# Latent attention: the order of the second head's products and the place of the exponential table load

## The chip, the cores and the metric

The kernel runs on one core of one Trainium2 chip. The metric is the device time of one execution in microseconds (us). The engines are TensorE (PE, with its weight loads shown apart as PEld), VectorE (DVE), ScalarE (ACT), GpSimd (POOL) and SyncE (SP, which here only issues the loads of weights).

## The reference, cut to what matters

Two layers of a trunk over 512 tokens of width 1024. Each layer normalises, runs three token mixers side by side (neighbourhood attention, latent attention, windowed attention with sinks), gates and adds them, projects out, and then runs a convolutional feed-forward block. The change touches the latent attention and the start of the feed-forward block's down projection:

```python
def mla_attention(c_q, c_kv, k_rope, g_qa, g_kva, w_uq, w_ukv, cos, sin):
    q = (rmsnorm(c_q, g_qa) @ w_uq).reshape(B, S, H, MLA_QK)      # 4 heads, 128 + 64 wide
    q_nope, q_pe = q[..., :128], apply_rope(q[..., 128:], cos, sin)
    kv = (rmsnorm(c_kv, g_kva) @ w_ukv).reshape(B, S, H, 256)
    k_nope, v = kv[..., :128], kv[..., 128:]
    ...
        s = (qn @ k_nope + qp @ k_pe) * scale                     # per block of 128 queries, per head
        p = softmax(s)
        return p @ v

def conv_ffn(h, w_up, conv_w, conv_b, w_down):
    ...
    return (gelu(g) * a) @ w_down

for l in range(2):
    h = rmsnorm(x, norm1_g[l]); x = x + gated_parallel_mixer(h, ...)
    h = rmsnorm(x, norm2_g[l]); x = x + conv_ffn(h, ...)
```

The gates are sigmoid(h @ w_gate + b), which the kernel computes with a hyperbolic tangent.

## The kernel before, in words

Every float32 product is made of three matmuls on split operands (a high part and a low part, lines 161 to 163): ACT casts the high part (line 147) and DVE subtracts it to get the low part (line 148). Weights come through a ring: three raw tiles (`raw`), three tiles of high parts (`whi`) and three of low parts (`wlo`). The method `weights` hands out the next weight and calls `fetch`, which writes down the load and the split of a weight three steps ahead; so these splits stand in the program where an earlier weight is taken, and they carry a priority 300 steps ahead of their place.

The order of PE and of SP is written out by hand: `schedule` builds a list of items, and `run` calls `do_` plus the item's name for each. The instructions of ACT and DVE are put in order by a planner when the kernel is built: it takes, by its own clock, the earliest instruction in the program among those whose inputs are there, with a bonus of 300 steps for weight splits and of 100 for the items of attention (`ATTN`). On the chip each engine then runs its list strictly in that order.

The part that the change touches, in the order of PE before:

- `qr`: the rotary queries of all four heads. `rope` and `stack` (lines 210 to 220) turn each pair of heads into four tiles `qr`.
- `("qn", 0)` and `("kn", 0)`: the first head's queries and keys, 9 and 6 matmuls. `do_kn` scales the keys into `ev` (line 154) and then splits them (lines 147, 148).
- a gate, 24 matmuls into one PSUM bank. DVE empties that bank with one multiply (`gz`, line 154), and ACT runs the tangent (line 664).
- `("qn", 1)` and `("kn", 1)`: the second head's queries and keys, 9 and 6 matmuls.
- `("ms", 0, 0)` and `("ms", 0, 1)`: the first head's scores, two tiles of 128 queries each; a tile is 5 matmuls (lines 490 to 494). Then DVE finds the row maximum (`nm`, line 496), ACT the exponential (line 498), DVE the reciprocal (line 499), and ACT scales (line 500).
- another gate, 24 matmuls.

The scores have three PSUM banks, 2, 3 and 4 (`s=[2, 3, 4]` in `do_mla_attn`), handed out in turn, so the fourth tile takes bank 2 again and has to wait until the first tile's exponential has read it. Ahead of that, the products of `lat4`, `kr`, `v`, `qr`, `qn`, `kn` and the gate take the banks 4, 5, 0, 1, 2, 3 in turn, by which the gate's product lies in bank 2. So the first tile of scores has to wait until `gz` has emptied bank 2. `mla_attn` only hands out the banks anew and issues nothing.

The build puts a table load into ACT's list ahead of the first instruction that needs another table than the one loaded. The trace has four of them, and none ahead of a tangent, which runs after either of the two tables. One is at the start (line 85, before a small exponential on a column of ones), one at the first gelu of each layer (line 851), and one at the first exponential of the second layer's latent attention (line 498).

Of the kernel before, what the change touches and what calls it, by code (L numbers as in the profile page):

```python
# [13 lines left out]
AF = mybir.ActivationFunctionType  # L14
# [28 lines left out]
def r32(ap):  # L43
    return ap.bitcast(F32)
# [14 lines left out]
class Trunk:  # L59
# [5 lines left out]
    def __init__(self, ctx, tc, d):  # L65
        self.tc, self.nc, self.d, self.ctx = tc, tc.nc, d, ctx
        nc = self.nc
        self.small = ctx.enter_context(tc.tile_pool(name="small", bufs=1))
        self.const = ctx.enter_context(tc.tile_pool(name="const", bufs=1))
        self.wp = ctx.enter_context(tc.tile_pool(name="wp", bufs=1))  # L70
        self.psum = ctx.enter_context(tc.tile_pool(name="psum", bufs=1, space=bass.MemoryType.PSUM))
        self.groups, self.turn = {}, {}
        c = self.const
        self.x = [c.tile([P, S], F32, name=f"x{k}") for k in range(KD)]
        self.par = [self.small.tile([P, NPC], F32, name=f"par{l}") for l in range(L)]
        nc.scalar.dma_start(self.par[0], d["par"][0])
        self.early = c.tile([P, P], F32, tag="acc", name="early")
        nc.vector.memset(self.early, 1.0)
        self.idf = c.tile([P, P], F32, name="idf")
        make_identity(nc, self.idf)  # L80
        cst = self.small.tile([P, 6], F32, name="cst")
        self.neghalf, self.ones = cst[:, 0:4], cst[:, 4:5]
        nc.vector.memset(self.neghalf, -0.5)
        nc.vector.memset(self.ones, 1.0)
        nc.scalar.activation(cst[:, 5:6], self.ones, AF.Exp)
        self.idb = self.small.tile([P, P], BF16, name="idb")
        nc.vector.tensor_copy(self.idb, self.idf)
        self.specs, self.raws, self.parts, self.used = [], [], [], 0
        self.plans = [self.schedule(l) for l in range(L)]
        for s, W in self.plans:  # L90
            self.specs += [w for item in s for w in W.get(item, ())]
        nc.sync.dma_start(self.x[0], d["xT"][0:P, :])
        self.fetch(1, 0)
        for k in range(1, KD):
            if k == 4:
                self.fetch(3, 0)
            nc.sync.dma_start(self.x[k], d["xT"][k * P:(k + 1) * P, :])
        self.gmask = self.small.tile([P, 2 * P], BF16, name="gmask")
# [138 lines left out]
    def schedule(self, l):  # L237
        d = self.d
        w_in, w_uq, w_ukv = d["w_in"][l], d["w_uq"][l], d["w_ukv"][l]
        W = {}  # L240
        halves = lambda w, cs: [(w, 512 * hf, 4, c, P) for hf in range(2) for c in cs]
        W["lat"] = halves(w_in, [OFF_CQ + i * P for i in LAT])
        W["lat4"] = [(w_in, 0, KD, OFF_CQ + 4 * P, P)]
        W["kr"] = [(w_in, 0, KD, OFF_KR, 64)]
        W["v", 0] = [(w_ukv, 0, 2, 512, 512)]
        W["qr"] = [(w_uq, 0, 3, 512, 256)]
        for h in range(4):
            W["qn", h] = [(w_uq, 0, 3, h * P, P)]
            W["kn", h] = [(w_ukv, 0, 2, h * P, P)]
        for p in range(4):  # L250
            for i, n in enumerate("qkv"):
                W["na" + n, p] = [(w_in, 0, KD, 512 * i + p * P, P)]
        W["gk"] = [(w_in, 0, KD, OFF_GK, P)]
        W["gv"] = [(w_in, 0, KD, OFF_GV, P)]
        for i in range(4):
            W["gq", i] = [(w_in, 0, KD, OFF_GQ + i * P, P)]
        for b in range(3):
            for m in range(KD):
                W["gate", b, m] = [(w_in, 0, KD, OFF_GATE + b * D + m * P, P)]
                W["br", b, m] = [(d["w_br"][b][l], 0, 4, m * P, P)]  # L260
        W["br012"] = W["br", 2, 0] + W["br", 2, 1] + W["br", 2, 2]
        W["out"] = halves(d["w_out"][l], [m * P for m in range(4)])
        for m in range(4, KD):
            W["out", m] = [(d["w_out"][l], 0, KD, m * P, P)]
        ups = [p * NF + f for f in range(NF) for p in range(2)]
        W["up"] = halves(d["w_up"][l], [f * P for f in ups[:4]])
        for f in ups[4:]:
            W["up", f] = [(d["w_up"][l], 0, KD, f * P, P)]
        for g in range(2):
            W["down", g] = [(d["w_down"][l], k0 * P, nk, (4 * g + m) * P, P)  # L270
                            for k0, nk in ((0, 8), (8, 8), (16, 6)) for m in range(4)]

        gate = iter([("gate", b, m) for b in (1, 0, 2) for m in range(8)]).__next__
        s = ["mla_open", "lat", "lat4", "rs_q", "kr", "rb_q", "rs_k", ("v", 0), ("v", 1), "rb_k", "qr"]
        s += [("qn", 0), ("kn", 0), gate(), "mla_attn", ("qn", 1), ("kn", 1), ("ms", 0, 0), ("ms", 0, 1), gate()]
        for h in range(3):
            dn = [("qn", h + 2), ("kn", h + 2)] if h < 2 else [("naq", 0)]
            s += [("ms", h + 1, 0), ("mt", h, 0)] + dn + [("mp", h, 0), ("mt", h, 1), ("ms", h + 1, 1), ("mp", h, 1)]
        s += [gate(), ("mt", 3, 0), ("nak", 0), ("mp", 3, 0), ("mt", 3, 1), ("nav", 0), ("mp", 3, 1)]
        s += ["na_open", ("nvt", 0), ("ns", 0), ("naq", 1), ("ns", 1), ("nav", 1), ("br", 1, 0), ("nt", 0)]  # L280
        s += [("nak", 1), ("np", 0), ("nt", 1), ("br", 1, 1), gate(), ("np", 1)]
        for p in (1, 2):
            h = 2 * p
            s += [("nvt", p), ("ns", h), ("naq", p + 1), ("ns", h + 1), ("nav", p + 1), ("nt", h)]
            s += [("nak", p + 1), ("np", h), ("nt", h + 1), ("br", 1, p + 1), gate(), ("np", h + 1)]
        s += [("nvt", 3), ("ns", 6), ("br", 1, 4), gate(), ("ns", 7), ("br", 1, 5), gate(), ("nt", 6)]
        s += [("br", 1, 6), gate(), ("np", 6), ("nt", 7), ("br", 1, 7), gate(), ("np", 7)]
        s += ["gq_open", "gk", ("gq", 0), "gv", ("gq", 1), "gvt", gate(), ("br", 0, 0), ("br", 0, 1)]
        s += [("gs", 0, 0), ("gq", 2), ("gs", 0, 1), ("gq", 3)]
        for i in range(7):  # L290
            s += [("gt", i, 0), ("gt", i, 1), ("gs", i + 1, 0), ("br", 0, i + 1) if i else gate(), ("gp", i)]
            s += [("gs", i + 1, 1), gate()]
        s += [("gt", 7, 0), ("gt", 7, 1), gate(), ("gp", 7), "br012", ("br", 2, 3)]
        for m in range(4, 8):
            s += [gate(), ("br", 2, m)]
        s += ["out"] + [("out", m) for m in range(4, KD)]
        s += ["up"] + [("up", f) for f in ups[4:]]
        s += [("down", 0), ("down", 1)]
        return s, W
# [558 lines left out]
    def do_down(self, g):  # L858
        nc = self.nc
# [4 lines left out]
        ps = [self.bank("g") for _ in range(4)]  # L864
        last = self.l == L - 1
        if g == 0 and not last:
            self.norm_begin()
        if g == 0 and last:
            self.acc, self.ntags, self.xg = None, ["acc", "sq0", "sq1"], []
# [169 lines left out]
```

## Time and profile before

| | us |
|---|---|
| median of 3 runs | 1739.96 |
| lowest and highest of them | 1739.75, 1740.38 |
| the profiled execution | 1738.54 |
| its span, first to last instruction | 1736.7 |
| PE busy in the span | 1720.7 |
| DVE, ACT busy | 1157.6, 860.8 |

The profile is of one execution. Its rows give the start and the length of instructions from the span's start. Matmuls are pipelined: a matmul of 512 columns is 0.39 us long in the rows, but the next one starts some 0.23 us after it; that step is called a slot below. A number in square brackets is the idle time of the engine ahead of the instruction, and what ended it.

### The profile page before, as it was taken

The page shows a single profiled execution, that of the slowest core. Times are in us where ns is not written, and L with a number is a line of the kernel's source. Part 1 is how long each engine was busy: PE and PEld are TensorE (multiplying, and loading weights), DVE is VectorE, ACT ScalarE, POOL GpSimd, SP SyncE. Part 2 cuts the span into 40 slices and gives each one's busy share as a digit, 9 for nine tenths or more (in the row PEclk, how much of TensorE's full clock was granted, in tenths as well). Part 3 has the DMA queues.
Part 4 walks back from the last instruction along what each step waited for, and adds up shares of the span by engine and source line. Part 5 has one row for each costly group of instructions (what it writes and reads, how often), then busy time and mean ns, then how long its engine had stood idle before and what let it go on. Part 6 is the DMA issues. An engine that isn't in the chain of part 4 may idle for free.

```text
span 1736.7 us, 21596 instructions
## 1 busy us (share of the span) xinstructions
PE 1720.7 (99%) x8146; PEld 1431.7 (82%) x8146; DVE 1157.6 (67%) x1872; ACT 860.8 (50%) x1499; POOL 35.2 (2%) x90
## 2 busy tenths in 40 slices
PE   9999999999999999999999999999999999999998
PEld 7788888888888888888887888888888888888887
DVE  6767875887558777734357688768765587777234
ACT  5865655664345444423248656456644354444232
POOL 1010000000000000000010100000000000000000
PEclk9999999999999999999999999999999999999999
DMA  5222233222333333333232232332233333333231
GB/s 174 70 81 79 80 92 85 73 68 68 97 98 109 97 97 97 97 89 106 80 85 76 73 89 67 109 86 61 62 85 104 93 108 98 97 98 97 85 103 67
DMA packets 290696, 155.40 MB, mean 89 GB/s; under 512 B 8672, under 2 KB 287072, under 8 KB 290592
## 3 DMA queue, kind: packets, MB, share of 16 engines
q1 hardware_dynamic: 288288, 148.92, 30.1%
q0 software_dynamic: 2016, 4.72, 0.9%
q8 instruction: 64, 1.05, 0.3%
q10 hardware_dynamic: 288, 0.38, 0.1%
q14 instruction: 40, 0.33, 0.1%
HBM read 151.89 MB, written 2.10 MB: 89 GB/s over the span
## 4 chain that ended last, share of the span: by engine, by line
PE 93%; DVE 3%; ACT 2%; issue 1%; DMA 0%; SPq 0%; POOLq 0%; POOL 0%; DVEq 0%; ACTq 0%
PE ps_d L161 21%; PE ps_d L162 20%; PE ps_d L163 20%; PE ps_g L162 7%; PE ps_g L163 7%; PE ps_g L161 7%; PE ps_po L648 1%; PE ps_tp L783 1%; PE ps_tp L634 1%; DVE wlo L148 1%; PE ps_tp L507 1%; ACT rsw L210 1%; PE ps_s L755 1%; PE ps_s L616 0%; PE ps_d L422 0%
## 5 line engine op out<-in xcount | busy, mean ns | idle before, releaser
L147 ACT CAST whi<-raw 128x1024 fp32r<-128x1024 f32 (+4 forms) x340 | 302.4, 890 | 615.5 <-PE ps_d L162 341.1
L161 PE MATMUL ps_d<-hh,whi 128*128 128x512 f32 x1328 | 520.5, 392 | 0.0
L163 PE MATMUL ps_d<-hh,wlo 128*128 128x512 f32 x1328 | 517.4, 390 | 0.3 <-DVE wlo L148 0.3
L162 PE MATMUL ps_d<-hl,whi 128*128 128x512 f32 x1328 | 516.9, 389 | 0.0
L148 DVE TENSOR_TENSOR wlo<-raw,whi 128x1024 fp32r<-128x1024 f32 (+4 forms) x338 | 345.1, 1022 | 199.1 <-ACT whi L147 198.8
L163 PEld LDWEIGHTS ps_d<-hh,wlo 128*128 128x128 f32 x1328 | 249.3, 188 | 53.6 <-DVE wlo L148 1.2
L161 PEld LDWEIGHTS ps_d<-hh,whi 128*128 128x128 f32 x1328 | 249.5, 188 | 50.5 <-DVE rot L154 0.6
L162 PEld LDWEIGHTS ps_d<-hl,whi 128*128 128x128 f32 x1328 | 249.5, 188 | 50.1
L161 PE MATMUL ps_g<-ff,whi 128*128 128x512 f32 x334 | 129.9, 389 | 0.0
L162 PE MATMUL ps_g<-ff,whi 128*128 128x512 f32 x334 | 129.9, 389 | 0.0
L163 PE MATMUL ps_g<-ff,wlo 128*128 128x512 f32 x334 | 129.9, 389 | 0.0
L154 DVE TENSOR_TENSOR u<-ps_d,rb 128x512 f32<-128x512 f32 x80 | 55.3, 692 | 64.6 <-PE ps_d L163 64.6
L154 DVE TENSOR_TENSOR gz<-ps_d,rb 128x512 f32<-128x512 f32 x48 | 33.2, 692 | 81.4 <-PE ps_d L163 81.2
L845 ACT ACTIVATE c<-u,par 128x512 f32<-128x512 f32 x88 | 71.9, 817 | 4.8 <-DVE u L154 2.8
L162 PEld LDWEIGHTS ps_g<-ff,whi 128*128 128x128 f32 x334 | 62.7, 188 | 13.1
L148 DVE TENSOR_TENSOR pl<-ps_tp,ph 128x512 fp32r<-128x512 f32 x104 | 69.0, 684 | 6.7 <-ACT ph L147 6.6
L161 PEld LDWEIGHTS ps_g<-ff,whi 128*128 128x128 f32 x334 | 62.7, 188 | 13.0
L163 PEld LDWEIGHTS ps_g<-ff,wlo 128*128 128x128 f32 x334 | 62.7, 188 | 12.9
L847 DVE SCALAR_TENSOR_TENSOR c<-u,par,c 128x511 f32<-128x511 f32 x88 | 66.0, 751 | 2.7
L851 ACT ACTIVATE c<-c 128x512 f32<-128x512 f32 x44 | 27.8, 632 | 77.2 <-DVE c L847 77.2
L846 DVE SCALAR_TENSOR_TENSOR c<-u,par,c 128x511 f32<-128x511 f32 x88 | 65.6, 746 | 0.6 <-ACT c L845 0.6
L147 ACT CAST ph<-ps_tp 128x512 fp32r<-128x512 f32 x104 | 57.6, 586 | 5.9 <-PE ps_tp L507 2.8
(286 smaller groups left out, 2651.5 us busy)
## 6 DMA issues: line engine op xcount, KB each, us to landing
raw<-in_w_in_dram SPq DMA_DIRECT2D x86, 512.0 KB, 4.0
raw<-in_w_up_dram SPq DMA_DIRECT2D x80, 512.0 KB, 3.8
raw<-in_w_down_dram SPq DMA_DIRECT2D x32, 512.0 KB, 3.8
raw<-in_w_down_dram SPq DMA_DIRECT2D x16, 384.0 KB, 3.3
raw<-in_w_in_dram SPq DMA_DIRECT2D x18, 256.0 KB, 2.9
raw<-in_w_br_mla_dram SPq DMA_DIRECT2D x16, 256.0 KB, 2.8
raw<-in_w_br_na_dram SPq DMA_DIRECT2D x16, 256.0 KB, 2.8
raw<-in_w_br_gqa_dram SPq DMA_DIRECT2D x16, 256.0 KB, 2.8
```

The costliest lines, as they stand in the source:

```text
L147: nc.scalar.copy(hi, src)
L148: nc.vector.tensor_sub(lo, src, r32(hi))
L154: self.nc.vector.tensor_tensor(out, a, b, ALU.mult)
L161: mm(ps, sh, mh, start=first and k == 0, stop=False)
L162: mm(ps, sh, ml, start=False, stop=False)
L163: mm(ps, sl, mh, start=False, stop=last and k == n - 1)
L210: nc.scalar.copy(sw[32 * i:32 * i + 32, :], ps[32 * j:32 * j + 32, :])
L507: self.nc.tensor.transpose(tp[:, b * P:(b + 1) * P], self.pts[h, b][:, kc * P:(kc + 1) * P], self.idf)
L845: nc.scalar.activation(c, u, AF.Identity, bias=pr[:, PC_CB + fi:PC_CB + fi + 1], scale=cw[:, 1:2])
L846: nc.vector.scalar_tensor_tensor(c[:, 1:], u[:, :S - 1], cw[:, 0:1], c[:, 1:], ALU.mult, ALU.add)
L847: nc.vector.scalar_tensor_tensor(c[:, :S - 1], u[:, 1:], cw[:, 2:3], c[:, :S - 1], ALU.mult, ALU.add)
L851: nc.scalar.activation(c, c, AF.Gelu_apprx_tanh)
```

## The change

In `schedule`, the first half of the first head's scores, `("ms", 0, 0)`, moves ahead of `("qn", 1)` and `("kn", 1)`; the second half stays behind them. This holds in both layers. In `do_down`, once in the kernel (first layer, first half of the down projection), ACT is given an exponential on one column. Its input is the last gelu product's high part, multiplied by zero, and its output is a column that nothing reads. `self.warm` names the column that the exponential at the start already wrote to.

```diff
-        nc.scalar.activation(cst[:, 5:6], self.ones, AF.Exp)
+        self.warm = cst[:, 5:6]
+        nc.scalar.activation(self.warm, self.ones, AF.Exp)
...
-        s += [("qn", 0), ("kn", 0), gate(), "mla_attn", ("qn", 1), ("kn", 1), ("ms", 0, 0), ("ms", 0, 1), gate()]
+        s += [("qn", 0), ("kn", 0), gate(), "mla_attn", ("ms", 0, 0), ("qn", 1), ("kn", 1), ("ms", 0, 1), gate()]
...
         if g == 0 and not last:
+            nc.scalar.activation(self.warm, r32(self.ff[-1][0])[:, 0:1], AF.Exp, scale=0.0)
             self.norm_begin()
```

## Rows read from the trace of the kernel before

**Rows 1.** The page: busy time of each engine, share of the span, instructions.

```profile
PE 1720.7 (99%) x8146; PEld 1431.7 (82%) x8146; DVE 1157.6 (67%) x1872; ACT 860.8 (50%) x1499; POOL 35.2 (2%) x90
```

**Rows 2.** Waits of PE: tile, releaser: total us, times, longest us.

```profile
PE ps_s L490 <- ACT pt L498: 4.3, 2, 2.6
...
PE ps_s L490 <- DVE gz L154: 0.5, 2, 0.2
```

**Rows 3.** Timeline of PE, first layer: start, length, instruction, [idle before].

```profile
61.21 0.39 PE L163 MATMUL ps_d<-hh,wlo 128*128 128x512 f32 x1
...
64.61 0.39 PE L163 MATMUL ps_d<-yah,wlo 128*128 128x512 f32 x1
65.24 0.47 PE L490 MATMUL ps_s<-kn,qn 128*128 128x512 f32 x1 [0.25 <-DVE gz L154]
...
67.60 0.39 PE L490 MATMUL ps_s<-kn,qn 128*128 128x512 f32 x1
...
70.54 0.50 PE L490 MATMUL ps_s<-kn,qn 128*128 128x512 f32 x1 [1.65 <-ACT pt L498]
...
71.80 0.39 PE L161 MATMUL ps_d<-hh,whi 128*128 128x512 f32 x1
```

**Rows 4.** Timeline of PE, the same place in the second layer.

```profile
923.32 0.47 PE L490 MATMUL ps_s<-kn,qn 128*128 128x512 f32 x1 [0.24 <-DVE gz L154]
...
925.71 0.39 PE L490 MATMUL ps_s<-kn,qn 128*128 128x512 f32 x1
...
929.61 0.50 PE L490 MATMUL ps_s<-kn,qn 128*128 128x512 f32 x1 [2.61 <-ACT pt L498]
...
930.88 0.40 PE L161 MATMUL ps_d<-hh,whi 128*128 128x512 f32 x1
```

**Rows 5.** Timeline of DVE, first layer, around the first tile of scores.

```profile
61.52 1.41 DVE L220 TENSOR_TENSOR qr<-rot,qr 64x512 fp32r<-64x512 f32 x2
62.96 0.69 DVE L148 TENSOR_TENSOR kn<-ev,kn 128x512 fp32r<-128x512 f32 x1
63.69 0.69 DVE L220 TENSOR_TENSOR qr<-rot,qr 64x512 fp32r<-64x512 f32 x1
64.41 0.69 DVE L154 TENSOR_TENSOR gz<-ps_d,rb 128x512 f32<-128x512 f32 x1
...
65.85 1.70 DVE L148 TENSOR_TENSOR wlo<-raw,whi 128x1024 fp32r<-128x1024 f32 x2
...
68.99 1.28 DVE L496 TENSOR_REDUCE nm<-ps_s 128x1 f32<-128x512 f32 x2
```

**Rows 6.** Timeline of DVE, the same multiply in the second layer.

```profile
922.48 0.69 DVE L154 TENSOR_TENSOR gz<-ps_d,rb 128x512 f32<-128x512 f32 x1
```

**Rows 7.** Timeline of ACT, second layer: the table load and the first exponential.

```profile
927.49 1.28 ACT L498 ACT_TABLE_LOAD   x1
928.78 0.69 ACT L498 ACTIVATE pt<-ps_s,nm 128x512 f32<-128x512 f32 x1
```

**Rows 8.** Timeline of ACT, first layer, start of the down projection.

```profile
752.35 0.62 ACT L147 CAST ff<-c 128x512 fp32r<-128x512 f32 x1
756.83 1.06 ACT L147 CAST whi<-raw 128x1024 fp32r<-128x1024 f32 x1 [3.87 <-PE ps_g L162]
```

**Rows 9.** Timeline of PE: the second gate's last matmul.

```profile
77.02 0.39 PE L163 MATMUL ps_d<-hh,wlo 128*128 128x512 f32 x1
```

**Rows 10.** Timeline of DVE: the multiply that empties that gate's bank.

```profile
77.45 0.69 DVE L154 TENSOR_TENSOR gz<-ps_d,rb 128x512 f32<-128x512 f32 x1 [3.07 <-PE ps_d L163]
```

**Rows 11.** Stretches: engines' busy us (instructions), granted PE clock, DMA share, GB/s.

```profile
928.50:929.00 0.50, 0.00 (x0) 0.00 (x0) 0.50 (x2) 0.49 (x2) 0.00 (x0) 1.00 0.41 112
...
1733.00:1733.50 0.50, 0.00 (x0) 0.00 (x0) 0.00 (x0) 0.00 (x0) 0.00 (x0) 0.97 0.98 385
1733.50:1734.00 0.50, 0.00 (x0) 0.00 (x0) 0.00 (x0) 0.00 (x0) 0.00 (x0) 0.50 0.96 369
```

**Rows 12.** Timeline of PE: its last matmuls in the span.

```profile
1729.58 0.74 PE L920 MATMUL ps_a<-idf,xg 128*128 128x128 f32 x5
```

## The prediction

> **What bounds the kernel now.** I first read the page's busy shares: PE is busy 1720.7 of 1736.7 us, so only 16.0 us of the span can be won at all, and every change that takes no work from PE must win out of these [rows 1]. The change takes no matmul away, so the next view is the list of PE's waits. It names little: the largest is 4.3 us in two waits of a score tile for an exponential, with 0.5 us in two waits of a score tile for the multiply that empties the gate's bank [rows 2]. Both stand in the stretch that the change reorders, once in each layer, so the third view is the timeline of that stretch, on PE and on DVE. (A matmul of 512 columns takes a slot: from 61.21 to 64.61 there are 15 steps, 0.227 us each [rows 3].)
>
> In the first layer the gate's last matmul starts at 61.21, the products of the second head fill the time to 64.61, and the first score tile starts at 65.24, not at 64.84. The fourth tile comes at 70.54 instead of 68.74, which is 67.60 plus five slots, and the second gate at 71.80 [rows 3]. Between the end of the first gate (the slot after 61.21 is 61.44) and 71.80 PE has 35 matmuls, 7.94 us of work, in 10.36 us: 2.4 us are lost, 0.4 ahead of the first tile, 1.8 ahead of the fourth, and the rest in the slower first slots after a wait. In the second layer the same stretch has the longer wait, 2.61 us against 1.65 [rows 3, 4].
>
> Why does it wait? DVE is working without a break there. After the gate's last matmul it still has two `qr` parts, the low part of `kn` and a third `qr` part ahead of the multiply `gz`, which runs from 64.41 to 65.10; PE's first score tile follows at 65.24, 0.14 us after it [rows 3, 5]. Then come two low parts of weights, and the first row maximum only at 68.99, although its scores were there some two us earlier [rows 5]. So PE's waits here are a backlog of DVE, which the 15 matmuls of the second head hide in part. In the second layer the backlog is the same (`gz` from 922.48 to 923.17, the tile at 923.32), and a table load of 1.28 us stands between the maximum and the first exponential on top of it [rows 4, 6, 7].
>
> **The change part by part.**
>
> *The table load.* The new exponential in the down projection brings one table load (1.28 us [rows 7]) and one instruction on one column, and the load at line 498 goes. The last gelu product's high part ends at 752.97 and ACT's next work starts at 756.83, after 3.87 us without any [rows 8]; 1.3 us and the small exponential (a few tenths) fit in there. Should they come one cast later, that cast makes weights for a product two weights on, over 10 us away at 24 slots a weight. I cost it at nothing. If that cover were gone it would cost at most its own length, 1.5 us. In the second layer the load's 1.28 us go from the wait ahead of the fourth score tile. On its own this part would win up to the difference of the two layers' waits, 2.61 - 1.65 = 1.0 us [rows 3, 4]. With the reorder that wait is gone in both layers, so the gain may not be counted twice.
>
> *The wait ahead of the fourth tile.* The second head's 15 matmuls, 3.4 us, now stand between the second and the third tile. The first tile's exponential thus has until 15 + 5 slots after the second tile's end. After the first tile's scores DVE has the last `qr` part and one weight's low part, some 1.8 us [rows 5], then the maximum, and ACT the exponential, 0.69 us each [rows 5, 7]; that is before the third tile even starts. This wait goes, in both layers. What is late next is the second head's keys, which are used only after the second gate's 24 slots, 5.4 us: hidden.
>
> *The wait ahead of the first tile.* Here the change takes away the cover. The first tile now stands directly behind the gate, and its bank is the one that holds the gate's product. It cannot start before `gz` has read that bank, and the low part of `kn` and the first `qr` part are needed within three slots more. All work of DVE ahead of `gz` was there already, and none of it depends on the matmuls that moved. The splits of the second head's own weights are taken from the program at the same places as before, since `weights` is called in the same order. So I see nothing that would make the planner put `gz` elsewhere, and take it where it is: the first tile starts at 65.24 and 923.32 as before, but PE now stands still from 61.44, for 3.8 us, with everything behind it in PE's list. Nobody else waits for longer, since ACT and DVE are working off what they had.
>
> *The sum.* First layer: 65.24, plus 2.36 us for two tiles (67.60 - 65.24), plus 3.40 us for 15 slots, plus 2.27 us for two more tiles, gives 73.27 for the second gate, against 71.80 [rows 3]: 1.47 us later. Second layer: 923.32 + 2.39 + 3.40 + 2.27 = 931.38 against 930.88 [rows 4]: 0.50 us later. Together +2.0 us, the gain of the table load included. The profiled execution of 1738.54 (span 1736.7 and 1.8 around it) would become 1740.5; the median of the runs shown stands 1.4 us above that execution, so I forecast 1739.96 + 2.0 = 1741.9 us. That is 0.11% slower, less than the 0.2% (3.5 us) which a measurement of this kernel can tell from no change.
>
> *The bounds.* The unknown is when `gz` ends. From below: if DVE ran it as soon as the gate is done. At the second gate, where DVE is free, the last matmul starts at 77.02 and the multiply at 77.45, and it takes 0.69 us [rows 9, 10]; with the 0.14 us to the next matmul the first tile would start 1.26 us after 61.21, a wait of 1.0 us instead of 2.4 and 3.4 lost: -1.4 and -2.4, in all -3.8 us. From above: `gz` behind one more DVE instruction of 0.69 us in each layer [rows 5], +1.4 us on top of +2.0. I take the place it has before, because its rows are of this very stretch.
>
> **The rivals.**
>
> *The clock of PE falls in the longer gap (slower).* PE would have no matmul from 61.60 (61.21 + 0.39) to 65.24, 3.6 us, in each layer. The gap of 2.6 us in the second layer was survived: the granted clock reads 1.00 in it [rows 11]. At the end of the span PE's last matmuls end at 1730.32, and the clock reads 0.97 in 1733.0 to 1733.5 and 0.50 after that [rows 11, 12], the lower of the two levels. The new gap is as long as the idle stretch in which it fell there. If it falls, each slot takes twice as long, 0.227 us more (an estimate, from the two levels). No row shows how soon it would rise: between none and all 35 slots to the second gate, 0 to 7.9 us in a layer. I take the ten slots of the two tiles behind the gap, 2.3 us: +4.3 us with one layer hit, 1744.3 us, and +6.6 with both, 1746.5 us. It decides where the gap has no matmul for longer than the one survived. Against it: neither gap is fixed to when the clock is looked at, so it may fall in one layer or execution and not in another.
>
> The Trainium skill, "TensorE: Matmul & The Clock Gate", Part 1, says that the throttled state is the default and that activity releases it, and it advises against idle gaps between bursts of matmuls. The end of this trace agrees, the gap inside it does not yet show a fall. By that rule this change trades two short gaps for one long one, which is the wrong way.
>
> *The planner puts the multiply early (faster).* If in the planner's list `gz` comes before the later `qr` parts, directly behind the first one, PE waits some 1.6 us for it and a few tenths for `kn`'s low part: about 1.9 us in each layer against 2.4 and 3.4, so -2.0 us, 1738 us; with everything needed ahead of it, -3.8 us, 1736.2 us. For it: the list already has `gz` ahead of a `qr` part that is older in the program, so the order depends on small times. Against it: all that stands ahead of it is older, and independent of what moved.
>
> *The change does not do what it says.* If the table load stays at the first exponential of the second layer, the sum is the same, because the fourth tile's wait is covered by 3.4 us; only a load at another place on the path would cost, up to 1.3 us: 1743 us.
>
> **How the numbers follow.** The forecast (the wait ahead of the first tile grows to 3.8 us, the clock holds, +1 to +3 us with small shifts of the planner's order) has 0.52. The clock falling in at least one layer has 0.26, the early multiply 0.17, the table load on the path 0.05. Of the early multiply a bit over half reaches -3.5 us, so faster by over 0.2% gets 0.10. The clock case passes +3.5 us nearly always, and shifts of order in the forecast sometimes do: slower by over 0.2% gets 0.28. The rest, 0.62, is within 0.2%. The range goes from 1736.8, which leaves out the far end of the early multiply, to 1746.0, which leaves out a fall in both layers.
>
> **What would show it.** Right: one wait of about 3.6 us of the first score tile for `gz` in each layer in place of 0.25, no wait of a score tile for an exponential, the first tile at about 65.2, the second gate at about 73.3, and the table load at about 753 with no wait of PE beside it. Wrong: a first tile at 62.5 to 63.5 (early multiply); slots of over 0.4 us behind the gap and a granted clock below 1.00 there (clock); a wait for the exponential still there (the cover is too short); a table load in the second layer's attention. If waits elsewhere change by more than one us, my assumption of an unchanged order of DVE has failed.

## The result

| | us | against the kernel before |
|---|---|---|
| kernel before, median of 7 | 1739.75 | |
| changed kernel, median of 7 (1743.37 to 1745.98) | 1745.0 | ratio 1.0031, 95% interval 1.0022 to 1.0040 |
| changed kernel, profiled execution (span 1741.6) | 1743.37 | |

The change makes the kernel slower by 0.31%, some 5 us. The forecast was 2 us slower, with the range to 1746.0; the first rival, that PE's clock falls because of the longer gap, is what happened, in the profiled execution in both layers.

The page of the changed kernel, busy time of each engine, against [rows 1]:

```profile
span 1741.6 us, 21597 instructions
...
PE 1722.7 (99%) x8146; PEld 1433.2 (82%) x8146; DVE 1157.6 (66%) x1872; ACT 860.7 (49%) x1500; POOL 35.2 (2%) x90
```

The matmuls are the same 8146, DVE has the same work and ACT one instruction more, but the span is 4.9 us longer. Of these, 2.0 are busy time of PE: the same matmuls took longer.

PE's waits in the changed kernel (tile, releaser: total, times, longest), against [rows 2]. Lines of the code from 86 on stand one further down than before, and those behind the new exponential (line 868) two:

```profile
PE ps_s L491 <- DVE gz L155: 7.3, 2, 3.7
PE ps_s L756 <- ACT pt L766: 1.4, 2, 0.7
```

The wait for an exponential is gone, and the wait for the multiply that empties the gate's bank has grown from 0.5 to 7.3 us. PE's timeline in the first layer, against [rows 3]:

```profile
61.10 0.39 PE L164 MATMUL ps_d<-hh,wlo 128*128 128x512 f32 x1
...
65.13 0.47 PE L491 MATMUL ps_s<-kn,qn 128*128 128x512 f32 x1 [3.64 <-DVE gz L155]
65.44 0.45 PE L492 MATMUL ps_s<-kn,qn 128*128 128x512 f32 x1
65.69 0.63 PE L493 MATMUL ps_s<-kn,qn 128*128 128x512 f32 x1
66.11 0.63 PE L494 MATMUL ps_s<-kr,qr 128*128 128x512 f32 x1
...
69.08 0.39 PE L162 MATMUL ps_d<-mg,whi 128*128 128x512 f32 x1
...
74.76 0.39 PE L162 MATMUL ps_d<-hh,whi 128*128 128x512 f32 x1
```

The same place in the second layer, against [rows 4]:

```profile
922.27 0.39 PE L164 MATMUL ps_d<-hh,wlo 128*128 128x512 f32 x1
...
926.31 0.77 PE L491 MATMUL ps_s<-kn,qn 128*128 128x512 f32 x1 [3.65 <-DVE gz L155]
926.87 0.63 PE L492 MATMUL ps_s<-kn,qn 128*128 128x512 f32 x1
...
930.04 0.39 PE L162 MATMUL ps_d<-mg,whi 128*128 128x512 f32 x1
...
935.73 0.39 PE L162 MATMUL ps_d<-hh,whi 128*128 128x512 f32 x1
```

A matmul that was 0.39 us long is 0.63 us long behind the gap, and the next one starts 0.43 us after it instead of 0.23. The stretches of the changed kernel (length, busy time of PE, PEld, DVE, ACT and POOL with the number of instructions, then the granted clock) say why:

```profile
62.00:65.00 3.00, 0.00 (x0) 0.00 (x0) 2.86 (x5) 2.37 (x4) 0.00 (x0) 1.00 0.18 43
...
65.60:69.00 3.40, 3.40 (x9) 2.67 (x9) 2.02 (x3) 0.92 (x3) 0.00 (x0) 0.51 0.19 57
69.00:72.00 3.00, 3.00 (x14) 2.45 (x14) 0.92 (x3) 1.99 (x5) 0.00 (x0) 0.99 0.00 1
...
925.00:926.00 1.00, 0.00 (x0) 0.00 (x0) 0.97 (x2) 0.61 (x1) 0.00 (x0) 0.90 0.00 0
...
925.70:929.20 3.50, 2.89 (x7) 2.34 (x8) 2.76 (x4) 0.72 (x1) 0.00 (x0) 0.51 0.03 5
```

The clock falls to the lower level, 1.2 GHz, about when PE has work again. In the first layer it is at its full level all through the wait and falls some 0.5 us after the first matmul (65.13). In the second it falls within the wait, ahead of the first matmul (926.31): from 925.00 to 926.00 PE has none, and the mean of the clock is 0.90 already. Some 3.4 us of work in the first layer are done at half speed, 2.9 in the second.

From the first gate's last matmul to the second gate's first there are 13.66 us (74.76 - 61.10) where there were 10.59 [rows 3], and in the second layer 13.46 us (935.73 - 922.27) where there were 11.60 (that gate's last matmul was at 919.28, the second gate at 930.88 [rows 4]). Together +4.93 us: the whole difference of the two spans. The row of the kernel before:

```profile
919.28 0.39 PE L163 MATMUL ps_d<-hh,wlo 128*128 128x512 f32 x1
```

DVE's multiply (first and second layer) against [rows 5] and [rows 6], and ACT at the start of the down projection against [rows 8]:

```profile
64.29 0.69 DVE L155 TENSOR_TENSOR gz<-ps_d,rb 128x512 f32<-128x512 f32 x1
...
925.47 0.69 DVE L155 TENSOR_TENSOR gz<-ps_d,rb 128x512 f32<-128x512 f32 x1
```

```profile
755.34 0.62 ACT L148 CAST ff<-c 128x512 fp32r<-128x512 f32 x1
755.98 1.28 ACT L868 ACT_TABLE_LOAD   x1
757.27 0.20 ACT L868 ACTIVATE cst<-ff 128x1 f32<-128x1 f32 x1
759.83 1.05 ACT L148 CAST whi<-raw 128x1024 fp32r<-128x1024 f32 x1 [2.35 <-PE ps_g L163]
```

The multiply ends 0.15 us ahead of the first score tile, as before, behind the same DVE instructions. The table load went where it was meant to go, and ACT still waits 2.35 us behind it.

### The profile page after: what moved, and what is told of

It reads as the page before. It is cut to its first block, busy times and chain, and to the rows that moved or that the text cites. A ratio compares the mean times of both kernels' runs of the same rounds, so it can differ in the third digit from the quotient of the medians.

```text
span 1741.6 us, 21597 instructions
## 1 busy us (share of the span) xinstructions
PE 1722.7 (99%) x8146; PEld 1433.2 (82%) x8146; DVE 1157.6 (66%) x1872; ACT 860.7 (49%) x1500; POOL 35.2 (2%) x90
## 4 chain that ended last, share of the span: by engine, by line
PE 93%; DVE 3%; ACT 2%; issue 1%; DMA 0%; SPq 0%; POOLq 0%; POOL 0%; DVEq 0%; ACTq 0%
PE ps_d L162 20%; PE ps_d L163 20%; PE ps_d L164 20%; PE ps_g L163 7%; PE ps_g L162 7%; PE ps_g L164 7%; PE ps_po L649 1%; ACT rsw L211 1%; PE ps_tp L784 1%; PE ps_tp L635 1%; PE ps_tp L508 1%; DVE wlo L149 1%; ACT whi L148 1%; PE ps_s L756 0%; PE ps_s L617 0%
```

## The experiments

The theory: the new order lays bare a wait for the gate's bank that the second head's products had covered (+2.0 us with the table load's gain taken off), and PE's clock falls because of the idle time, which costs the rest. The rivals: the slow matmuls have another cause, or the table load is not where its gain was counted. Each kernel ran beside the kernel before on the same chip.

**Only the table load.** The changed kernel with the old order.

```diff
-        s += [("qn", 0), ("kn", 0), gate(), "mla_attn", ("ms", 0, 0), ("qn", 1), ("kn", 1), ("ms", 0, 1), gate()]
+        s += [("qn", 0), ("kn", 0), gate(), "mla_attn", ("qn", 1), ("kn", 1), ("ms", 0, 0), ("ms", 0, 1), gate()]
```

> Only the exponential in the down projection; the order of the products is the old one. Theory (the table load stood in the second layer's wait ahead of the fourth score tile, and nowhere else on PE's path): that wait falls from 2.61 us to about the first layer's 1.65, and the time by about 1.0 us against the kernel before; the load itself shows in the down projection with no wait of PE beside it. Rival (the new load costs something in the down projection, or the second layer's longer wait has another cause): no gain, or a loss of up to 1.5 us.

Measured 1737.02 us against 1739.34 (median of 32), ratio 0.9988 (0.9979 to 0.9997). PE's longest wait in this kernel, and then the second layer's fourth tile in PE's timeline:

```profile
PE ps_s L491 <- ACT pt L499: 3.2, 2, 1.6
```

```profile
928.10 0.50 PE L491 MATMUL ps_s<-kn,qn 128*128 128x512 f32 x1 [1.61 <-ACT pt L499]
```

The wait is 1.61 us in both layers, as the theory said. But the gain is 2.3 us, not 1.0. The mean granted clock of each execution, known to three places, accounts for it. I read 0.999 as an execution whose only fall is at the very end, 0.998 as one fall more, 0.997 and 0.996 as two, or one that lasts. The nine profiled executions agree with this; for the others it is inferred:

| kernel | executions | 0.999 | 0.998 | 0.997, 0.996 |
|---|---|---|---|---|
| before | 32 | 10 (median 1738.01) | 21 (1739.54) | 1 (1740.14) |
| before, beside the kernels with 7 matmuls or a fourth bank | 15 | 7 (1738.19) | 6 (1739.66) | 2 (1741.13) |
| changed | 7 | 0 | 0 | 7 (1745.0) |
| only the table load | 11 | 11 (1737.02) | 0 | 0 |
| only the order | 10 | 0 | 0 | 10 (1744.03) |
| 14 matmuls in the gap | 11 | 11 (1739.88) | 0 | 0 |
| 7 matmuls in the gap | 11 | 3 (1739.81) | 6 (1741.51) | 2 (1742.90) |
| banks 3, 4, 2 | 11 | 2 (1736.67) | 7 (1738.10) | 2 (1739.72) |
| fourth bank | 5 | 5 (1733.26) | 0 | 0 |
| fourth bank, 3, 4, 2, table load | 5 | 5 (1732.18) | 0 | 0 |

So the kernel before already loses its clock in about two of three executions (30 of all 47), mostly once, for 1.5 us (1739.54 - 1738.01). No kept trace shows such a fall, since its profiled execution is one of those without. That the fall belongs to the wait of 2.61 us follows from this kernel, in which only that wait is much shorter. Against its executions without a fall the table load alone wins 1.0 us (1738.01 to 1737.02), the number expected; the other 1.3 us of the medians are the fall, which occurs in none of this kernel's 11 executions, behind waits of 1.61 us.

**Only the order.** The changed kernel without the exponential in the down projection.

```diff
-            nc.scalar.activation(self.warm, r32(self.ff[-1][0])[:, 0:1], AF.Exp, scale=0.0)
```

> Only the new order; the exponential in the down projection is left out. Theory (with the new order the first exponential of the second layer has 3.4 us of cover, so the table load is hidden there): the same time as the changed kernel, about 5 us above the kernel before, within 0.5 us; the table load is back at the second layer's first exponential, and no score tile waits for an exponential. Rival (the load is still on the path, and the order alone costs more than the sum of both): about 1 us slower than the changed kernel.

Measured 1744.03 us, ratio 1.0026 (1.0016 to 1.0035). That is 1.0 us below the changed kernel, outside the 0.5 that I allowed, but the two intervals overlap, and it is not the slower time that the rival wanted. ACT's timeline in the second layer, then the stretch behind PE's wait there:

```profile
926.86 1.28 ACT L499 ACT_TABLE_LOAD   x1
929.47 0.69 ACT L499 ACTIVATE pt<-ps_s,nm 128x512 f32<-128x512 f32 x1 [1.33 <-DVE nm L497]
```

```profile
925.20:932.00 6.80, 5.76 (x14) 4.54 (x15) 4.32 (x7) 4.24 (x7) 0.00 (x0) 0.50 0.11 31
```

The load is back, and ACT is idle for 1.33 us between it and the exponential. Under the new order the load's place makes no difference that these runs can tell; the order alone makes the loss. The clock fell in both layers of this execution too. In the second it was low for twice as long, and again from within the wait: the first score tile starts at 926.24.

**The gap filled.** The changed kernel with matmuls that nothing reads, ahead of the first tile.

```diff
     def do_ms(self, h, half):
         nc, mm = self.nc, self.nc.tensor.matmul
+        if (h, half) == (0, 0):
+            idle = self.psum.tile([P, S], F32, tag="b7", name="idle")
+            for _ in range(14):
+                mm(idle, self.h[0][0][:, 0:P], self.h[0][0], start=True, stop=True)
```

> The changed kernel with 14 more matmuls of 512 columns (3.2 us of PE) into an unused PSUM bank, ahead of the first head's first score tile in each layer. They fill most of the idle time that the new order makes and delay nothing: the first tile still waits for the gate's bank, to about 65.1 and 926. Theory (of the 5 us about 2.0 are the longer wait, and 2.9 are slots at the half clock behind it): the granted clock stays at 1.00, the slots behind are 0.23 us, and the time is about 2.9 us below the changed kernel, 2.0 above the kernel before. Rival (the slow slots come from the operands or from the pressure on PSUM, not from the idle time): the slots of the first tiles stay at 0.43 us and the time stays 5 us above the kernel before.

Measured 1739.88 us, ratio 1.0005 (0.9996 to 1.0014). PE's timeline in the first layer of this kernel:

```profile
60.48 0.39 PE L164 MATMUL ps_d<-hh,wlo 128*128 128x512 f32 x1
60.70 3.33 PE L491 MATMUL idle<-hh 128*128 128x512 f32 x14
64.51 0.47 PE L495 MATMUL ps_s<-kn,qn 128*128 128x512 f32 x1 [0.48 <-DVE gz L155]
64.82 0.40 PE L496 MATMUL ps_s<-kn,qn 128*128 128x512 f32 x1
...
72.53 0.39 PE L162 MATMUL ps_d<-hh,whi 128*128 128x512 f32 x1
```

The first tile starts 4.03 us after the gate's last matmul, as in the changed kernel (65.13 - 61.10), but the matmuls behind it are at full speed, and the clock held in all 11 executions. From gate to gate it is 12.05 us; the sum of the prediction gives 12.06 (73.27 - 61.21). Against the executions of before without a fall the time is 1.9 us longer (1739.88 against 1738.01): the forecast's +2.0 is the cost of the order and the table load while the clock holds. Adding 3.2 us of useless work to PE in each layer makes the changed kernel some 5 us faster. I had expected 2.9: the 1.6 and 1.3 us that the falls cost in the changed kernel's profiled execution, which is the fastest of its seven. Against their median the falls cost 5.1 us (1745.0 - 1739.88).

**Half of the gap filled.** The same with 7 matmuls.

> The changed kernel with 7 more matmuls of 512 columns ahead of the first head's first score tile, half as many as before, so that the idle stretch behind them is about 2.0 us long in each layer and the first tile starts when it did. Theory (how long PE has no matmul in that stretch decides how often the clock falls): 2.0 us lies between the waits of 1.6 us, behind which it held in all executions, and the 2.6 us, behind which it fell in two thirds; so it falls in fewer executions than in the changed kernel, with 1740 to 1741.5 us for most, and more often than with 14 matmuls. Rival (any wait at this place drops the clock): both layers in every execution, 1743 us and more.

Measured 1741.5 us, ratio 1.0013 (1.0004 to 1.0022). PE's wait is 2.1 us in both layers:

```profile
61.03 1.75 PE L491 MATMUL idle<-hh 128*128 128x512 f32 x7
64.85 0.77 PE L495 MATMUL ps_s<-kn,qn 128*128 128x512 f32 x1 [2.07 <-DVE gz L155]
65.41 0.63 PE L496 MATMUL ps_s<-kn,qn 128*128 128x512 f32 x1
...
925.86 0.47 PE L495 MATMUL ps_s<-kn,qn 128*128 128x512 f32 x1 [2.06 <-DVE gz L155]
```

In this one execution the clock fell in the first layer and held in the second, behind waits of the same length. Over 11 executions it fell not at all, once or twice (table above), in steps of some 1.5 us, between the two kernels on either side, as the theory said. Whether it falls is not decided by the kernel alone.

**Another bank for the first tile.** The changed kernel with the first tile in bank 3.

```diff
-        self.banks(d=[0, 1], s=[2, 3, 4], tp=[5, 6], po=[7])
+        self.banks(d=[0, 1], s=[3, 4, 2], tp=[5, 6], po=[7])
```

> The changed kernel with the score tiles' banks handed out as 3, 4, 2 instead of 2, 3, 4, so that the first tile's bank is not the one that the gate's product lies in; the third tile gets that one. Theory (the first tile waits for the multiply only because of the bank): its first matmul starts as soon as the high part of the keys is there, about 62.3, its second with their low part at about 63.7, no idle stretch is longer than about 1 us, the clock holds, and the time is about 6.4 us below the changed kernel and 1.5 us below the kernel before. Rival (the backlog of DVE would hold the tile up by any bank, through the queries and keys that it still has to make): the tile starts at about 65 all the same, the clock falls, and the time is that of the changed kernel.

Measured 1738.1 us, ratio 0.9995 (0.9987 to 1.0004), about 7 us below the changed kernel. PE's waits in this kernel, then its timeline in the first layer (the gate's last matmul is at 60.55 here), then a stretch behind it, with the granted clock as the third number from the end:

```profile
PE ps_s L492 <- DVE kn L149: 1.7, 2, 0.8
PE ps_s L491 <- ACT kn L148: 1.5, 2, 0.8
```

```profile
61.70 0.50 PE L491 MATMUL ps_s<-kn,qn 128*128 128x512 f32 x1 [0.76 <-ACT kn L148]
63.05 0.75 PE L492 MATMUL ps_s<-kn,qn 128*128 128x512 f32 x1 [0.85 <-DVE kn L149]
```

```profile
63.00:66.40 3.40, 3.35 (x8) 2.68 (x9) 3.28 (x5) 1.60 (x2) 0.00 (x0) 0.52 0.00 0
```

Half of the theory holds: the tile starts 1.15 us after the gate's last matmul and waits for the keys alone, so it was the bank that held it. The other half fails: I expected the clock to hold with no wait over 1 us, and it fell in 9 of 11 executions, here behind two waits of 0.76 and 0.85 us with one matmul between them. In the two executions without a fall the time is 1736.67, 1.3 below the kernel before without one; expected was 1.5. Over all its executions the kernel cannot be told from the kernel before.

**A fourth bank, in the old order.** The kernel before, with the fourth tile in a bank that is free at that time.

```diff
-            s = self.bank("s")
+            s = self.bank("po" if (h, b) == (0, 3) else "s")
```

> The kernel before with one thing changed: the first head's fourth score tile takes the PSUM bank of the later products (bank 7, unused until then) and does not wait for bank 2. Neither the order nor the table load is touched. Theory (the fourth tile waits for the bank alone, and the clock falls in two thirds of the executions of the kernel before because of that wait): the waits of 1.65 and 2.61 us are gone, the granted clock holds in every execution, and the time is about 4.5 us below the executions of the kernel before in which the clock held (1738.0), so 1733.5 us, and 5.8 below its median. The second layer's table load is then hidden. Rival (the backlog of DVE is only handed on): the wait comes back at the second head's scores or at the first head's transposes, and the gain is under 2 us.

Measured 1733.26 us, ratio 0.9967 (0.9955 to 0.9980). PE's wait for the multiply in this kernel, and then the fourth tile (`ps_po`) in its timeline, a slot behind the third:

```profile
PE ps_s L490 <- DVE gz L154: 0.5, 2, 0.3
```

```profile
68.66 0.39 PE L490 MATMUL ps_po<-kn,qn 128*128 128x512 f32 x1
```

No score tile of the latent attention waits for an exponential any more, and no new wait has come in its place. The clock held in all five executions. Expected was 1733.5. The gain over the kernel before that ran beside it is 6.1 us by the medians, 4.9 at equal clock (1738.19).

**Fourth bank, banks 3, 4, 2 and the table load, in the old order.** The two edits of banks above, on the kernel with only the table load.

> The old order of the products, with the exponential in the down projection, the fourth tile in bank 7 and the banks of the other three in the order 3, 4, 2. Theory: beside the fourth tile's wait, the wait of 0.25 us ahead of the first tile goes too, with its slower first slots, 0.4 us in each layer; the table load is hidden either way and brings nothing more. So about 0.8 us below the kernel with the fourth bank alone, 1732.7 us. Rival (the first tile then waits for the keys or queries at the same time): the same as the kernel with the fourth bank alone.

Measured 1732.18 us, ratio 0.9962 (0.9949 to 0.9976). In this kernel PE is busy through the whole stretch:

```profile
61.00:64.00 3.00, 3.00 (x15) 2.49 (x14) 2.88 (x5) 2.95 (x5) 0.00 (x0) 1.00 0.22 63
64.00:67.00 3.00, 3.00 (x15) 2.47 (x14) 2.94 (x5) 1.61 (x4) 0.00 (x0) 1.00 0.00 0
67.00:70.00 3.00, 3.00 (x15) 2.48 (x14) 3.00 (x6) 1.67 (x4) 0.00 (x0) 1.00 0.51 132
```

This is the fastest of the kernels, 7.2 us below the kernel before and 12.8 below the changed kernel. It reaches by two banks what the change sought by an order. The further 1.1 us over the fourth bank alone are near the expected 0.8, but the intervals of the two overlap, and which of its two edits they belong to was not tried apart.

## Why the prediction was right or wrong

**Right: the wait ahead of the first tile.** It was said to be 3.6 us for `gz` with the first tile at 65.2; it is 3.64 us, at 65.13, since `gz` kept its place on DVE. The early multiply, the second rival, did not happen.

**Right: the wait ahead of the fourth tile goes.** It is in no list of waits of the changed kernel, and what was said to be late next, the second head's keys, holds up nothing.

**Right: the table load costs nothing in the down projection, and its gain may not be counted twice.** Alone it wins 1.0 us at equal clock; under the new order no gain shows.

**Right: the sum at full clock.** The kernel with the gap filled shows 12.05 us from gate to gate (12.06 forecast) and +1.9 us in all (+2.0 forecast).

**Wrong: which case was likeliest.** The forecast had the clock hold with 0.52 and gave its fall 0.26; a time slower by over 0.2% had 0.28, and 0.31% was measured. The clock fell in all 7 executions: in both layers of the profiled one, and the other six have the same mean clock or a lower one. The step that failed is the reading of the gap of 2.6 us as one that the clock survives [rows 11]. That was one execution, 1738.54 us, and one of the third in which the clock holds: in 30 of 47 executions of the kernel before it does not. The row could not tell, either: it lies within the gap, and in the changed kernel's first layer the clock reads 1.00 all through the gap and is low only behind it. A stretch behind the gap of the kernel before shows that in that execution the clock did hold:

```profile
930.00:932.00 2.00, 2.00 (x10) 1.64 (x9) 0.93 (x3) 2.00 (x6) 0.00 (x0) 1.00 0.21 62
```

**Wrong: the time that the sum was added to.** The median of 1739.96 stands 1.4 us above the profiled execution, and I carried that along as a constant. By the table above it is a fall of the clock, some 1.5 us. With a clock that holds, the sum starts from 1738.0 and gives 1740.0 us, as the kernel with the gap filled shows (1739.88), not 1741.9. Had I asked why the median lies above that execution, the rival would have had the larger chance.

**The price of the fall: near, though not for the reason given.** I took ten slots, 2.3 us in a layer. The profiled execution shows 1.6 us in the first layer (from 65.13 to 69.08 it is 3.95 us for the two tiles where 2.36 were counted) and 1.3 in the second (930.04 - 926.31 = 3.73 against 2.39): the clock is back after some eight matmuls, before the two tiles end. But that execution is the fastest of the seven. The median lies 5.1 us above the kernel with the gap filled, 2.6 in a layer. A fall of double length, as in the second layer of the kernel with only the order, would explain it (that execution has a mean clock of 0.996, as five of these seven do); no profile shows one of the changed kernel itself.

**Luck: the time lies in the range.** The range ended at 1746.0 to leave out a fall in both layers, which I had put at 1746.5. Such falls came, and 1745.0 is inside only because the start of the sum already held a fall: 1738.0 + 2.0 + 4.6 gives 1744.6.

**The rule of the Trainium skill, "TensorE: Matmul & The Clock Gate", Part 1,** that gaps between bursts let the clock fall back, was weighed against the row of one execution, and the row won. The runs bear the rule out: the change trades shorter waits for one longer wait, and more than half of what it loses against a held clock is the clock (2.9 of 4.9 us in the profiled executions, 5.1 of 7.0 by the medians). They also show falls behind shorter waits than the new one of 3.6 us, down to 2.1.

## What to carry to other kernels

Before moving work, ask what its old place covered: here the second head's products hid a wait for a PSUM bank, and a free bank removes the wait itself. A wait of PE can cost more than its length, because the matmuls behind it may run at half the clock; here that happened behind waits of 2.1 to 3.7 us, in some executions or in all. That one execution held its clock through a wait is no evidence that the next will, so look at the clock and the times of all of them. A table load is best hidden where ACT idles, but its gain counts only as long as its old wait is still on the path.

## What was not expected of the hardware

The clock fell behind two waits of 0.76 and 0.85 us with a single matmul between them (11 falls in the 22 stretches of the kernel with banks 3, 4, 2, counted by its executions' mean clocks), while it never fell behind a single wait of 1.61 us (none in the 22 stretches of the kernel with only the table load). So the length of the longest wait does not decide it, and the runs do not settle what does. Nor does a clock of 1.00 within a wait say that it will hold: in the changed kernel's first layer it reads 1.00 from 62.0 to 65.0, with no matmul, and 0.51 from 65.6 to 69.0, with PE at work. In the second layers of the changed kernel and of the one with only the order it fell ahead of the first matmul, within the wait.
